# Mixer A, prompt: two chunks of keys scored at once by two 64-row tiles of TensorE, three products each

## The chip, the cores and the metric

The kernel runs on one core of one Trainium2 chip. The metric is the device time of one launch in microseconds (us). Before the change the median of three runs is 1541.89 us (1539.67 to 1544.26).

## The reference, cut to what matters

Two token sequences, a prompt of 1024 and a sample of 512, pass through two layers with shared weights. In the first layer mixer A is dense attention with 8 query heads on 2 groups of keys and values, 64 numbers per head:

```python
def dense_gqa(q, k, v):
    ...
    def attend(qblk):
        s = jnp.einsum('bqkgd,bskd->bkgqs', qblk, k).astype(F32)
        p = jax.nn.softmax(s, axis=-1).astype(v.dtype)
        return jnp.einsum('bkgqs,bskd->bqkgd', p, v)
```

A block of 128 queries sees all keys of its own sequence: 1024 in the prompt, 512 in the sample. Everything is in 32-bit floats.

## The kernel before

**Two parts per number.** TensorE takes 32-bit data in a fast form (F32R) that keeps fewer bits. So the kernel splits an operand into a high part and a low part and adds products of parts. A projection with weights `w` and tokens `x` takes three F32R products per step (`proj_fm_k`): high by high, high by low, low by high.

**Scores of mixer A.** A head has 64 numbers, and the array of TensorE has 128 rows. The kernel stacks: the tile K of a key group (`ak`) holds the high part of the keys on partitions 0 to 63 and the low part on 64 to 127, and the query tiles `qh` and `ql` hold the high and the low part of a head twice, once per half. The product of `qh` with K is then high by high plus high by low, and that of `ql` with K the two others. So 512 keys cost two matmuls on all 128 rows.

**Units.** A unit is one block of 128 queries of one key group, with 4 heads. There are 2 groups and 12 blocks, the four of the sample first and then the eight of the prompt, for the first group and then for the second. `front_a` (L763) makes a unit's scores and exponentials. For a prompt block there are two chunks of 512 keys per head (`nh` is 2); each chunk takes one PSUM bank `s`, two matmuls (recorded at L89, the helper `mm`) and a row maximum on VectorE (L782). Then the smaller of the two negated maxima is taken (L787), ScalarE makes the exponentials (L790), VectorE the sums and their reciprocals (L792, L793), and GpSimd scales the exponentials (L107). The `yield` between the chunks ends a step of the pipeline.

**Products with the values.** `Back.T` (L628) transposes four blocks of exponentials into a bank `pte` (L170) and splits them into `eh` (ScalarE, L111) and `el` (VectorE, L112); `Back.PV` (L636) multiplies them with the values into `po`.

**The order of the work.** `pipeline` (L673) writes the program's order: after the transposes of a key block it takes as many steps of later units' `front_a` as the 12 exponential buffers and a credit allow, then some `fill` pieces, then the products of the key block before. Fills are the query projections of the second group (`psq`), the gate projections (`psg`), and later the out projection (`pso`). When the program is built, a scheduler puts the instructions of each engine into their final order: by priority, which follows the program's order, but an instruction whose buffer is not yet free in the scheduler's own clock waits aside while others go ahead. The five PSUM banks with tag `s` serve the scores, the transposes `pte` and the query transposes `ptq` alike.

**K in DRAM.** `kv_group` (L458) writes each key group to DRAM as 128 rows, high over low, 1024 keys wide for the prompt. `load_a` (L756) brings it back with one DMA from GpSimd's queue (L760).

**Another use of a half array.** In mixer B the scores `pss` are 32-bit products with 64 rows (`kT` by `qT`, four products of 128 columns, each recorded as two instructions); the products `kv` and mixer B's `po` beside them have the same columns on 128 rows. `b_proj` makes its projections `psb` (256 columns, F32R, 128 rows).

Of the kernel before, what the change touches and what calls it, by code (L numbers as in the profile page):

```python
# [9 lines left out]
F32R = mybir.dt.float32r  # L10
AF = mybir.ActivationFunctionType
ALU = mybir.AluOpType
AX = mybir.AxisListType
# [3 lines left out]
P = 128  # L17
# [19 lines left out]
def trunk_kernel(ctx, tc, x, xT, wab, woab, wc, woc, gT, qkg, ret, sink, relb, fng,  # L37
                 ropeA, ropeB, dist, kdist, qdist, onehot, wmask, out_p0, out_p1, out_s):
    nc = tc.nc
# [13 lines left out]
    def buf(tag, name, n=None, dt=F32):  # L53
        t = wk.tile([P, SIZE[tag]], dt, tag=tag, name=name, bufs=BUFS[tag])
        return t if n is None else t[:, :n]

    def ps_s(name):
        return pp.tile([P, 512], F32, tag="s", name=name, bufs=5)
# [14 lines left out]
    def small(name, n, bufs=2):  # L73
        return st.tile([P, n], F32, tag=name, name=name, bufs=bufs)
# [13 lines left out]
    def mm(ps, lhsT, rhs, start, stop):  # L88
        i = nc.tensor.matmul(ps, lhsT=lhsT, rhs=rhs, start=start, stop=stop)  # L89
        if pace["after"] is not None:  # L90
            tc.add_manual_dep(i.ins, pace["after"], order, reason="a filler keeps to its place in the pipeline")
            pace["after"] = None
        return i
# [12 lines left out]
    def scale_pool(o, i, s):  # L106
        nc.gpsimd.tensor_scalar(o, i, s, 1.0, ALU.mult, ALU.mult)  # L107
# [22 lines left out]
    def load_w(arr, c, tag, lo=None, hook=None, ks=range(KT)):  # L130
        ts = {}
        for i in (k // 2 for k in ks[::2]):
            raw = wp.tile([P, 2 * CW], F32, tag="wraw", name="wraw", bufs=2)
            dma(out=raw, in_=arr[c, :, 2 * i:2 * i + 2, :].rearrange("p k n -> p (k n)"))
            w = wp.tile([P, 2, 2 * CW], F32R, tag=tag, name=tag, bufs=4)
            nc.gpsimd.tensor_scalar(w[:, 0, :], raw, 1.0, 1.0, ALU.mult, ALU.mult)  # L136
            (lo or nc.gpsimd).tensor_tensor(w[:, 1, :], raw, w[:, 0, :].bitcast(F32), ALU.subtract)  # L137
            ts[i] = w
            if hook is not None:
                hook(i)  # L140

        def get(s, k, a=0, n=CW):
            o = (k % 2) * CW + a
            return ts[k // 2][:, s, o:o + n]
        return get
# [183 lines left out]
    def scratch(name):  # L329
# [8 lines left out]
    sp_d = {(n, g, i): dr.tile([P, 1024 if i == 0 else 512], F32, name=f"sp{n}{g}{i}")[:]  # L338
            for n in ("ak", "av", "ch", "cl", "cv") for g in range(2) for i in range(2)}

# [1 line left out]
    ident = const.tile([P, P], F32, name="ident")  # L342
    make_identity(nc, ident)
    nhalf = const.tile([P, 8], F32, name="nhalf")
# [16 lines left out]
        for b in range(t * GB, t * GB + GB):  # L361
            block_rstd(load_block(x[b], "xb", "H"), rs[:, b:b + 1])

# [1 line left out]
    dma(out=g_sb, in_=gT)  # L365
    nc.scalar.activation(rs, rs, AF.Tanh)
    wkv = load_w(wab, 4, "w", None, lambda i: [load_xt(0, k) for k in ((0, 1), (2, 3, 4, 5), (6, 7), ())[i]])
# [127 lines left out]
        if p % 2:  # L495
            kv_group(p // 2)

# [1 line left out]
    ropeb = buf("S4", "ropeb").rearrange("p (f b d) -> p f b d", f=2, b=8)  # L499
    dma(out=ropeb, in_=ropeB)  # L500
    qdec = buf("S4", "qdec").rearrange("p (h a i) -> p h a i", h=4, a=2)
# [116 lines left out]
            tail, last = retention(h, w, b0, b1), tail  # L618
            last()

# [1 line left out]
    class Back:  # L622
        def __init__(self, eget, n, vget, od, k0, t, j, gd):
            self.n, self.eget, self.vget, self.od, self.k0, self.t, self.j = n, eget, vget, od, k0, t, j
# [46 lines left out]
                split(X["h", k, self.t][:, sl], X["l", k, self.t][:, sl], oT[:, a, :], 0.5)  # L671

    def pipeline(units, prep, front, cap, frees, rate, fill, hook, before=None):  # L673
        """Software pipeline: the scores of later units run beside the products of this one, as far as
        the buffers of the exponentials (cap of them) reach."""
        n = len(units)
        st_ = dict(u=0, gen=None, live=0)
        ctxs, backs, pend = {0: prep(units[0])}, {}, []

        def advance():  # L680
            u = st_["u"]
            if u >= n:
                return False
            if st_["gen"] is None:
                st_["gen"] = front(units[u], ctxs.pop(u))
                if u + 1 < n:
                    ctxs[u + 1] = prep(units[u + 1])
                st_["need"] = next(st_["gen"])
            if st_["live"] + st_["need"] > cap:
                return False  # L690
            st_["live"] += st_["need"]
            try:
                st_["need"] = next(st_["gen"])
            except StopIteration as e:
                backs[u] = e.value
                st_["u"], st_["gen"] = u + 1, None
            return True

        credit = 0.0
        for u in range(n):  # L700
            while u not in backs:
                advance()
                if before is not None and backs:
                    before()
                    before = None
            back = backs.pop(u)
            for kb in range(back.n):
                back.T(kb)
                st_["live"] -= frees(kb, back.n)
                credit = min(credit + rate(back.n), 4.0)  # L710
                while credit >= 1.0 and advance():
                    credit -= 1.0
                fill.step()
                for f in pend:
                    f()
                pend = [lambda bk=back, kb=kb: bk.PV(kb)]
                if kb == 0:
                    hook(units[u])
        for f in pend:
            f()  # L720
# [33 lines left out]
    kv_a = {}  # L754

    def load_a(name, g, b):  # L756
        i = 0 if b < 8 else 1
        if (name, g, i) not in kv_a:
            kv_a[name, g, i] = buf(("S4", "S2")[i], name, None, F32R)
            nc.gpsimd.dma_start(out=kv_a[name, g, i], in_=sp_d[name, g, i])  # L760
        return kv_a[name, g, i]

    def front_a(u, ctx):  # L763
        g, b = u
        qh, ql = ctx
        t, j = b // GB, b % GB
        s0, s1 = (0, 8) if b < 8 else (8, 12)
        nh = (s1 - s0) // GB
        K = load_a("ak", g, b)
        nm, rl = small("nm", 4), small("rl", 4)  # L770
        l = small("l", 8).rearrange("p (h c) -> p h c", h=4)
        es = []
        for h in range(4):
            yield nh
            ss = []
            nm2 = small("nm2", 2, 4)
            for c in range(nh):
                kk = K[:, c * 512:(c + 1) * 512]
                s = ps_s("s")
                mm(s, qh[:, h * P:(h + 1) * P], kk, True, False)  # L780
                mm(s, ql[:, h * P:(h + 1) * P], kk, False, True)
                nc.vector.tensor_reduce(nm2[:, c:c + 1] if nh == 2 else nm[:, h:h + 1], s, AX.X, ALU.max, negate=True)  # L782
                ss.append(s)
                if c < nh - 1:
                    yield 0
            if nh == 2:
                nc.vector.tensor_tensor(nm[:, h:h + 1], nm2[:, 0:1], nm2[:, 1:2], ALU.min)  # L787
            eh = [buf("E", "e") for c in range(nh)]
            for c in range(nh):
                nc.scalar.activation(eh[c], ss[c], AF.Exp, bias=nm[:, h:h + 1], accum_out=l[:, h, c:c + 1])  # L790
            if nh == 2:
                nc.vector.tensor_tensor(rl[:, h:h + 1], l[:, h, 0:1], l[:, h, 1:2], ALU.add)  # L792
                nc.vector.reciprocal(rl[:, h:h + 1], rl[:, h:h + 1])  # L793
            else:
                nc.vector.reciprocal(rl[:, h:h + 1], l[:, h, 0:1])
            for c in range(nh):
                scale_pool(eh[c], eh[c], rl[:, h:h + 1])
            es.append(eh)
        return Back(lambda h, kb: es[h][kb // 4][:, (kb % 4) * P:(kb % 4 + 1) * P], s1 - s0,
                    lambda kb: load_a("av", g, b)[:, kb * P:(kb + 1) * P], o_ab, 2 * g, t, j,  # L800
                    g_ab if g == 1 and t < 2 else None)

# [1 line left out]
    def fin_fm(t, k, y, rb):  # L804
        nc.gpsimd.tensor_tensor(y, y, rb, ALU.mult)
        split_x(y, k, t, g_sb[:, KT + k:KT + k + 1])
# [22 lines left out]
    def begin():  # L829
# [3 lines left out]
        for _ in range(POST_A):  # L833
            fill.one()

    pipeline([(g, b) for g in range(2) for b in BLOCKS], prep_a, front_a, BUFS["E"],
             lambda kb, n: 4 if kb % 4 == 3 else 0, lambda n: 2.0, fill, hook_a, begin)
    drain(ahead)
# [11 lines left out]

    out_proj(1, woab, KS_A, lambda b: x[b], fin_ab)

# [1 line left out]
    wkv = load_w(wc, 0, "w")  # L854
    kd_raw = {}
    for p in PAIRS:
# [34 lines left out]
            split(q[r0:r0 + 64], q[r1:r1 + 64], ps[r0:r0 + 64], 0.125)  # L891
        yield

# [1 line left out]
    k_c, v_c = {0: (KH, KL)}, {0: (V,)}  # L895
    qs = {}
    bias_c = {}
# [104 lines left out]
        return Back(lambda h, kb: es[h][:, kb * P:(kb + 1) * P], k1 - k0, lambda kb: vget_c(c, k0 + kb), o_c, 2 * c, t, j,  # L1002
                    g_c if (c, t) == (3, 1) else None)

# [1 line left out]
    def fin_out(t, k, y, rb):  # L1006
        nc.vector.scalar_tensor_tensor(y, y, g_sb[:, 2 * KT + k:2 * KT + k + 1], rb, ALU.mult, ALU.mult)
        dma(out=(out_p0, None, out_s)[t][k], in_=y)
# [126 lines left out]
```

## Time and profile before

| | |
|---|---|
| median of 3 runs | 1541.89 us (1539.67 to 1544.26) |
| span of the profiled execution | 1541.9 us |
| TensorE matmul busy | 1467.9 us, 95% of the span |
| VectorE busy | 1061.1 us, 69% |
| GpSimd busy | 804.7 us, 52% |
| ScalarE busy | 714.0 us, 46% |
| mean granted TensorE clock | 0.985 |

Times are device microseconds. The profiled execution is one run of its own; its span agrees with the median of the timed runs. PE is TensorE's matmuls and PEld its weight loads, which run beside them; DVE is VectorE, ACT ScalarE, POOL GpSimd. Matmuls are pipelined: a 512-column matmul is shown with 0.39 us, of which neighbours overlap, so that the distance from start to start is the time that one costs. A shape such as 64\*128 in a row is the rows and columns of the array that an instruction uses.

### The profile page before, as it was taken

Reading aid. Unit: us, or ns where it says so; the run is one execution under the profiler, and the core shown is the slowest. Engines: PE = TensorE matmul, PEld = TensorE weight load, DVE = VectorE, ACT = ScalarE, POOL = GpSimd, SP = SyncE. Lnnn points to the kernel's source line nnn. Section 1 sums busy time; section 2 is a strip of 40 time slices with the busy share of each in tenths; the row PEclk is TensorE's granted clock in tenths of the full one; section 3 lists DMA queues with packets and bytes.
Section 4 is the critical chain, followed back from the end, with each engine's and each line's share of the span. In section 5 each row is a group of like instructions: output and inputs, shape, how many; then the busy total and the mean of one; then the engine's idle time right before and its main releaser. Section 6 shows DMA issues by size and latency. Waiting matters only on the chain.

```text
span 1541.9 us, 26034 instructions
## 1 busy us (share of the span) xinstructions
PE 1467.9 (95%) x8746; PEld 1277.2 (83%) x8746; DVE 1061.1 (69%) x2488; ACT 714.0 (46%) x1768; POOL 804.7 (52%) x1040
## 2 busy tenths in 40 slices
PE   7989999989999999999998999999999999988897
PEld 7988999987888888778777998888888888766677
DVE  6596455578667667877888327677777767898554
ACT  3632222245455555655653235556556556555102
POOL 7783334257456374887896414442522432567433
PEclk9998999999999999999999999999999999999999
DMA  9441011224421132654563422112213211567773
GB/s 334 155 154 52 19 45 49 64 85 140 138 73 59 48 110 73 217 166 130 153 218 115 124 78 78 52 57 56 80 49 93 61 53 52 169 211 235 242 247 123
DMA packets 112662, 179.54 MB, mean 116 GB/s; under 512 B 12880, under 2 KB 34000, under 8 KB 112528
## 3 DMA queue, kind: packets, MB, share of 16 engines
q1 hardware_dynamic: 110512, 172.37, 35.6%
q0 software_dynamic: 2016, 5.51, 1.2%
q8 instruction: 69, 1.13, 0.3%
q14 instruction: 65, 0.53, 0.1%
HBM read 125.63 MB, written 56.39 MB: 118 GB/s over the span
## 4 chain that ended last, share of the span: by engine, by line
PE 65%; DVE 12%; DMA 8%; POOL 5%; issue 4%; ACT 2%; SPq 1%; POOLq 0%; DVEq 0%; ACTq 0%
PE psg L89 16%; PE psq L89 10%; PE psb L89 8%; PE po L89 8%; PE pte L170 6%; PE pso L89 4%; PE sc L89 3%; PE s L89 3%; PE pskv L89 2%; DMA wraw<-in_woc 2%; DVE xl L118 1%; DVE w L137 1%; DVE nm L782 1%; DMA wraw<-in_woab 1%; DVE el L112 1%
## 5 line engine op out<-in xcount | busy, mean ns | idle before, releaser
L89 PE MATMUL psg<-xh,wg 128*128 128x512 f32 x768 | 261.6, 399 | 1.4 <-POOL wg L137 1.2
L112 DVE TENSOR_TENSOR el<-pte,eh 128x512 fp32r<-128x512 f32 x288 | 196.6, 684 | 56.7 <-ACT eh L111 29.6
L107 POOL TENSOR_SCALAR ec<-ec,rl 128x384 f32<-128x384 f32 (+1 forms) x192 | 109.0, 582 | 233.0 <-DVE rl L997 77.1
L111 ACT ACTIVATE eh<-pte 128x512 fp32r<-128x512 f32 x288 | 169.4, 596 | 119.6 <-PE po L89 66.4
L89 PE MATMUL pso<-xh,w 128*128 128x512 f32 x512 | 179.8, 409 | 9.8 <-DVE w L137 4.3
L89 PEld LDWEIGHTS psg<-xh,wg 128*128 128x128 f32 x768 | 143.7, 188 | 29.7 <-POOL wg L137 1.6
L107 POOL TENSOR_SCALAR e<-e,rl 128x512 f32<-128x512 f32 x160 | 114.6, 728 | 81.7 <-DVE rl L793 23.8
L89 PE MATMUL psg<-xl,wg 128*128 128x512 f32 x384 | 151.1, 393 | 0.0
L992 ACT ACTIVATE ec<-ec,nm 128x384 f32<-128x384 f32 (+1 forms) x192 | 109.6, 572 | 85.6 <-DVE nm L990 80.8
L790 ACT ACTIVATE e<-s,nm 128x512 f32<-128x512 f32 x160 | 108.9, 687 | 75.3 <-DVE nm L787 56.1
L136 POOL TENSOR_SCALAR w<-wraw 128x512 fp32r<-128x512 f32 x116 | 78.7, 680 | 117.7 <-DMA wraw<-in_woc 35.2
L782 DVE TENSOR_REDUCE nm<-s 128x1 f32<-128x512 f32 x160 | 107.5, 682 | 34.3 <-PE s L89 34.0
L89 PE MATMUL psq<-xh,w 128*128 128x512 f32 x384 | 130.1, 397 | 0.6 <-DVE oT L655 0.6
L89 PEld LDWEIGHTS pso<-xh,w 128*128 128x128 f32 x512 | 96.1, 191 | 34.7 <-DVE w L137 7.8
L986 DVE CUSTOM_DVE_ANT_0 ec<-sc,bias,sink_s 128x384 f32<-128x384 f32 (+1 forms) x192 | 105.2, 568 | 20.3 <-PE sc L89 17.4
L89 PE MATMUL pso<-xl,w 128*128 128x512 f32 x256 | 102.0, 399 | 3.3 <-DVE xl L118 3.3
L170 PEld LDWEIGHTS pte<-ident,e 128*128 128x128 f32 x640 | 78.4, 142 | 20.5 <-ACT e L790 1.7
L170 PE MATMUL pte<-ident,e 128*128 128x128 f32 x640 | 94.6, 275 | 0.8 <-ACT e L790 0.6
L137 POOL TENSOR_TENSOR w<-wraw,w 128x512 fp32r<-128x512 f32 x68 | 90.5, 1335 | 1.8
L89 PEld LDWEIGHTS psq<-xh,w 128*128 128x128 f32 x384 | 71.8, 188 | 14.4 <-PE po L89 0.9
L89 PEld LDWEIGHTS psg<-xl,wg 128*128 128x128 f32 x384 | 72.3, 188 | 13.2
L89 PE MATMUL pskv<-w,xh 128*128 128x256 f32 x384 | 73.3, 293 | 9.0 <-ACT xh L117 6.7
(225 smaller groups left out, 3981.8 us busy)
## 6 DMA issues: line engine op xcount, KB each, us to landing
wraw<-in_woab SPq DMA_DIRECT2D x48, 256.0 KB, 3.3
wraw<-in_woc SPq DMA_DIRECT2D x48, 256.0 KB, 3.6
wraw<-in_wab SPq DMA_DIRECT2D x44, 256.0 KB, 3.3
wraw<-in_wc SPq DMA_DIRECT2D x36, 256.0 KB, 3.2
xt<-in_xT SPq DMA_DIRECT2D x24, 256.0 KB, 5.3
xb<-in_x SPq DMA_DIRECT2D x24, 256.0 KB, 4.9
qd<-qdw SPq DMA_DIRECT2D x24, 256.0 KB, 2.0
qd<-qd SPq DMA_DIRECT2D x24, 256.0 KB, 3.1
```

Of the source, the lines that this page charges most:

```text
L89: i = nc.tensor.matmul(ps, lhsT=lhsT, rhs=rhs, start=start, stop=stop)
L107: nc.gpsimd.tensor_scalar(o, i, s, 1.0, ALU.mult, ALU.mult)
L111: nc.scalar.activation(hi, src, AF.Copy)
L112: nc.vector.tensor_tensor(lo, src, hi.bitcast(F32), ALU.subtract)
L118: nc.vector.scalar_tensor_tensor(lo, src, scale, hi.bitcast(F32), ALU.mult, ALU.subtract)
L136: nc.gpsimd.tensor_scalar(w[:, 0, :], raw, 1.0, 1.0, ALU.mult, ALU.mult)
L137: (lo or nc.gpsimd).tensor_tensor(w[:, 1, :], raw, w[:, 0, :].bitcast(F32), ALU.subtract)
L170: return nc.tensor.transpose(o, i, ident)
L782: nc.vector.tensor_reduce(nm2[:, c:c + 1] if nh == 2 else nm[:, h:h + 1], s, AX.X, ALU.max, negate=True)
L790: nc.scalar.activation(eh[c], ss[c], AF.Exp, bias=nm[:, h:h + 1], accum_out=l[:, h, c:c + 1])
L986: nc.vector.tensor_tensor_reduce(es[h][:, :nk], s, bias[h][:, bo:bo + nk], 1.0, sink_s[:, 4 * c + h:4 * c + h + 1], ALU.add, ALU.max, mx[: ...
L992: nc.scalar.activation(es[a][:, :nk], es[a][:, :nk], AF.Exp, bias=nm[:, a:a + 1], accum_out=l[:, a:a + 1])
```

## The change

For prompt blocks the K tile holds one chunk of 512 keys on partitions 0 to 63 and the other on 64 to 127, each with its high part (index 0) and its low part (index 1) side by side. Four DMAs of 64 rows by 512 keys replace one. A head then takes both banks at the start and issues six matmuls of 64 rows, alternating between the two halves of the array: high by high, high by low, low by high for each chunk. The fourth product, low by low, is left out for the prompt. Both maxima follow, and the `yield` between the chunks is gone. Sample blocks stay as they were.

```diff
     def load_a(name, g, b):
         i = 0 if b < 8 else 1
         if (name, g, i) not in kv_a:
-            kv_a[name, g, i] = buf(("S4", "S2")[i], name, None, F32R)
-            nc.gpsimd.dma_start(out=kv_a[name, g, i], in_=sp_d[name, g, i])
+            src = sp_d[name, g, i]
+            if name == "ak" and i == 0:
+
+                kk = buf("S4", name, None, F32R).rearrange("p (s k) -> p s k", s=2)
+                for r in range(2):
+                    for s in range(2):
+                        nc.gpsimd.dma_start(out=kk[64 * r:64 * r + 64, s, :],
+                                            in_=src[64 * s:64 * s + 64, 512 * r:512 * r + 512])
+                kv_a[name, g, i] = kk
+            else:
+                kv_a[name, g, i] = buf(("S4", "S2")[i], name, None, F32R)
+                nc.gpsimd.dma_start(out=kv_a[name, g, i], in_=src)
         return kv_a[name, g, i]
...
         for h in range(4):
             yield nh
-            ss = []
-            nm2 = small("nm2", 2, 4)
-            for c in range(nh):
-                kk = K[:, c * 512:(c + 1) * 512]
-                s = ps_s("s")
-                mm(s, qh[:, h * P:(h + 1) * P], kk, True, False)
-                mm(s, ql[:, h * P:(h + 1) * P], kk, False, True)
-                nc.vector.tensor_reduce(nm2[:, c:c + 1] if nh == 2 else nm[:, h:h + 1], s, AX.X, ALU.max, negate=True)
-                ss.append(s)
-                if c < nh - 1:
-                    yield 0
+            hs = slice(h * P, (h + 1) * P)
+            ss = [ps_s("s") for c in range(nh)]
             if nh == 2:
+
+                for n, (q, kl) in enumerate(((qh, 0), (qh, 1), (ql, 0))):
+                    for c in range(2):
+                        rows = slice(64 * c, 64 * c + 64)
+                        mm(ss[c], q[rows, hs], K[rows, kl, :], n == 0, n == 2)
+                nm2 = small("nm2", 2, 4)
+                for c in range(2):
+                    nc.vector.tensor_reduce(nm2[:, c:c + 1], ss[c], AX.X, ALU.max, negate=True)
                 nc.vector.tensor_tensor(nm[:, h:h + 1], nm2[:, 0:1], nm2[:, 1:2], ALU.min)
+            else:
+                mm(ss[0], qh[:, hs], K, True, False)
+                mm(ss[0], ql[:, hs], K, False, True)
+                nc.vector.tensor_reduce(nm[:, h:h + 1], ss[0], AX.X, ALU.max, negate=True)
```

The other hunks of the diff only turn comment lines and a docstring into blank lines.

## Rows read from the trace of the kernel before

**Rows 1.** The page, part 1: TensorE's busy time, share of the span, instructions.

```profile
PE 1467.9 (95%) x8746; PEld 1277.2 (83%) x8746; DVE 1061.1 (69%) x2488; ACT 714.0 (46%) x1768; POOL 804.7 (52%) x1040
```

**Rows 2.** Busy time by stretch: length, five engines, granted clock, DMA share, GB/s.

```profile
358.00:400.00 42.00, 38.88 (x201) 30.65 (x201) 29.96 (x70) 18.51 (x43) 22.56 (x28) 1.00 0.70 205
400.00:545.00 145.00, 143.85 (x734) 118.36 (x733) 97.31 (x203) 77.09 (x174) 76.04 (x94) 1.00 0.18 58
...
597.00:700.00 103.00, 97.27 (x483) 78.16 (x483) 83.53 (x150) 58.59 (x130) 74.76 (x78) 0.98 0.50 157
700.00:796.00 96.00, 93.86 (x474) 74.47 (x473) 81.47 (x155) 55.80 (x127) 81.33 (x86) 1.00 0.52 155
```

**Rows 3.** Chain of waits from 400 to 545 us, shares by line.

```profile
by line: PE psg L89 49.9%; PE s L89 14.8%; PE pte L170 14.5%; PE po L89 13.8%; DMA gab<-gz 10.8%; PE ptq L170 1.8%; DVE nm L787 1.6%; DVE nm L782 1.0%; issue 0.9%; ACT e L790 0.7%; ACT eh L111 0.4%; ACT th L213 0.0%; ACTq L213 0.0%
```

**Rows 4.** Tile s: count, duration ns min/median/max, first and last start us, forms.

```profile
L89 PE MATMUL s<-ak,qh x160: 387/395/796, 319.4 to 793.4; 128*128 128x512 f32 x160
...
L89 PE MATMUL s<-ak,ql x160: 387/394/628, 319.7 to 793.7; 128*128 128x512 f32 x160
L782 DVE TENSOR_REDUCE nm<-s x160: 661/681/693, 320.2 to 796.7; 128x1 f32<-128x512 f32 x160
```

**Rows 5.** Timeline of PE, two heads of one unit: start us, us, what.

```profile
423.84 0.39 PE L89 MATMUL s<-ak,qh 128*128 128x512 f32 x1
424.07 0.39 PE L89 MATMUL s<-ak,ql 128*128 128x512 f32 x1
424.30 0.63 PE L89 MATMUL psg<-xh,wg 128*128 128x512 f32 x2
...
425.69 0.39 PE L89 MATMUL s<-ak,qh 128*128 128x512 f32 x1
...
427.53 0.39 PE L89 MATMUL s<-ak,qh 128*128 128x512 f32 x1
```

**Rows 6.** Timeline of PE: first and last prompt head, starts of both chunks.

```profile
358.51 0.39 PE L89 MATMUL s<-ak,qh 128*128 128x512 f32 x1
...
358.98 0.39 PE L89 MATMUL s<-ak,qh 128*128 128x512 f32 x1
...
791.76 0.40 PE L89 MATMUL s<-ak,qh 128*128 128x512 f32 x1
...
793.38 0.50 PE L89 MATMUL s<-ak,qh 128*128 128x512 f32 x1 [0.22 <-DVE el L112]
```

**Rows 7.** Timeline of PE, mixer B, 180 to 185 us, around the 64-row products.

```profile
180.38 0.28 PE L89 MATMUL psb<-wg,xh 128*128 128x256 f32 x1
180.50 1.05 PE L89 MATMUL kv<-z,kfb 128*128 128x128 f32 x8
...
183.10 0.36 PE L89 MATMUL psb<-wg,xh 128*128 128x256 f32 x1
183.30 0.28 PE L89 MATMUL psb<-wg,xl 128*128 128x256 f32 x1
183.42 0.29 PE L89 MATMUL psb<-wg,xh 128*128 128x256 f32 x1
183.63 1.16 PE L89 MATMUL pss<-qT,kT 64*128 64x128 f32 x8
184.72 0.39 PE L89 MATMUL psb<-wg,xh 128*128 128x256 f32 x1
184.94 0.28 PE L89 MATMUL psb<-wg,xl 128*128 128x256 f32 x1
```

**Rows 8.** Timeline of PE's weight loads at the same place.

```profile
183.30 0.19 PEld L89 LDWEIGHTS psb<-wg,xh 128*128 128x128 f32 x1
183.63 0.96 PEld L89 LDWEIGHTS pss<-qT,kT 64*128 64x128 f32 x8
```

**Rows 9.** Tile pss: all 64-row products of mixer B.

```profile
L89 PE MATMUL pss<-qT,kT x96: 272/272/579, 122.9 to 298.4; 64*128 64x128 f32 x96
```

**Rows 10.** Tile ak: its loads, duration ns, first and last start us.

```profile
L760 POOL DMA_DIRECT2D ak<-spak x4: 540/628/771, 281.7 to 548.5; - x4
```

## The prediction

> **What bounds the kernel now.** I read the page first: TensorE's matmuls fill 95% of the span and no other engine passes 69% [rows 1]. Then the four stretches in which the prompt's scores of mixer A run: TensorE is busy 38.88 of 42 us, 143.85 of 145, 97.27 of 103 and 93.86 of 96, so only 3.1, 1.2, 5.7 and 2.1 us are idle, 12.1 in all [rows 2]. The chain of waits in the longest of them is nearly all TensorE, with the scores at 14.8% [rows 3]. So here a microsecond of TensorE's time is about a microsecond of the kernel, as long as it isn't put into that idle time. What counts is the distance from one matmul's start to the next, not the 0.39 us of one: in the timeline 512-column products follow each other every 0.23 us [rows 5].
>
> The trace has no pair of row tiles, but it has matmuls on half the rows. In mixer B eight instructions of 64 rows stand between projections of 128 rows [rows 7]. From the start of the last projection before them (183.42) to the start of the second one after them (184.94) are 1.52 us. The control stands just ahead: from 180.38 to 183.30 the same kind of projections enclose 24 instructions of the same 128 columns on 128 rows (the 8 shown and the 16 of `po`), in 2.92 us. A projection of 256 columns takes 0.12 us there (180.38 to 180.50, 183.30 to 183.42), so one of the 24 takes (2.92 - 2 x 0.12) / 24 = 0.112 us, with no extra at either end. Eight of 64 rows and two projections should take 8 x 0.112 + 2 x 0.12 = 1.13 us; they took 1.52. **A round trip from 128 rows to 64 and back costs 0.39 us.** The weight loads show where: up to there each is pulled ahead of its matmul, but after the load at 183.30 the first one of 64 rows starts only at 183.63, with its matmul [rows 8]. There are twelve such groups (96 instructions) [rows 9], always with projections around them. I call any such run of 64-row matmuls an island.
>
> **What the change removes and adds.** 16 prompt units of 4 heads are 64 heads, and each loses four full matmuls (of the 320 recorded [rows 4], 256 go): 4 x 0.23 = 0.92 us a head. Each gets six 64-row matmuls instead, three per chunk.
>
> *Do two tiles run at the same time?* No row shows it. The bounds are 0.23 us for a pair (full overlap) and 0.46 (none). I take overlap, since the operands lie on different rows and different banks, and add 0.11 us a head, because the second tile's weights are loaded behind the first's: the eight loads of 64 rows follow each other every (0.96 - 0.19) / 7 = 0.11 us [rows 8]. The Trainium skill ("TensorE: Matmul & The Clock Gate", Part 3) puts the offset of two tiles at some 4 ns instead. By that the sum below would be 24 x 0.11 = 2.6 us less, within its range.
>
> *Do a head's six stand together?* The program has them in one piece, but the scheduler lets an instruction whose bank isn't free wait aside while later ones go on. The first product of the second chunk needs a second bank; the other two of the first chunk don't. So where the second bank comes late, the first chunk's three products run alone, then projections, then the second chunk's three: nothing overlaps and there are two islands. How late it comes is seen in the order of before, which also asks for both chunks in one go: the chunks of two heads start at 423.84, 425.69, 427.53 and so on, with projections between [rows 5]. I measured the distance from chunk to chunk over all 64 heads, from the first (358.51 to 358.98) to the last (791.76 to 793.38) [rows 6]: 24 are within 1.0 us, and 40 lie 1.1 to 5.3 us apart. An island of three takes about 0.3 us to enter and 0.69 to run, so I take the 24 as together and the 40 as split. The bounds are all together and all split.
>
> Prices a head: together 3 x 0.23 + 0.11 + 0.39 = 1.19, which is 0.27 more than 0.92; split 2 x (3 x 0.23 + 0.39) = 2.16, which is 1.24 more. The price of an island is from 32-bit products of 128 columns. For F32R of 512 columns it could lie between nothing (rival 3) and 0.50 us, if the engine has to run empty and a matmul of 512 columns lasts 0.11 us longer than one of 256 (0.39 [rows 5] against 0.28 [rows 7]); over 24 + 80 islands that would be 11 us more. I take 0.39, since the projections around it are F32R and the control shows no extra for the change of type alone.
>
> **Sum:** 24 x 0.27 + 40 x 1.24 = 6.5 + 49.6 = 56 us more on TensorE. Of the 12.1 us idle I let half be filled: -6 (bounds 0 and -12). That is +50 us on the profiled 1541.9 us, which is also the median of the runs (1541.89): **1592 us**.
>
> **Edits costed at nothing.** The two more loads per product change nothing of their own: they are in the pitch. K for the prompt comes in four DMAs instead of one, twice, so six more issues at 0.63 us on GpSimd's queue, 3.8 us [rows 10]; behind them wait the scalings of the exponentials. GpSimd is idle in at least 15% of each stretch [rows 2] and the last load of K was issued at 548.5, some 50 us ahead of the stretch at 597 that uses it. Uncovered it would be the 3.8 us, plus a transfer at most. Both row maxima (0.68 us each [rows 4]) now come behind the third pair, so the exponentials start later by some 0.3 us a head; the scores run half a unit ahead of the transposes, with projections to fill. Without that cover it is 64 x 0.3 = 19 us. The lost `yield` moves no step: the credit of four took both chunks in one go before.
>
> **Rivals.**
> 1. *All heads together, pairs overlapping.* For it: the six are adjacent in the program. Against it: the chunks' distances [rows 5, 6]. 64 x 0.27 = 17 us, less 6: 1553 us (1547 to 1559). Still slower, since the island costs more than the saved slot.
> 2. *Tiles don't overlap.* A head together takes 6 x 0.23 + 0.39 = 1.77, 0.85 more; split heads stay. 24 x 0.85 + 49.6 - 6 = +64: 1606 us, at most 1621 (64 x 1.24, nothing filled).
> 3. *Faster.* The saved slot shows and the islands don't cost: three pairs plus 0.11 against four, 0.12 us a head, or 0.23 if the second load is hidden: 64 x that is 8 to 15 us, 1527 to 1534. It decides if a round trip costs under 0.12 (0.23) us between F32R matmuls of 512 columns and the six stay together. For it: the trace's price is from another type. Against it: rows 7 and the split. The Trainium skill ("TensorEngine Tiling", Theoretical Speedup) promises up to twice the speed for 64 rows, which would be this rival; but its Key Properties say that a change of tiling mode drains the engine, which is what rows 7 and 8 show.
> 4. *No change.* Heads A and B of a step are written one behind the other; if they make one island of twelve, 6 x 0.23 + 0.11 + 0.39 = 1.88 stands against 1.84: 32 x 0.04 = +1 us, 1543. Against it: they are 1.8 us apart now [rows 5].
>
> **How the numbers follow.** Forecast 0.50, with a range of its own from 1570 (24 split, all idle filled) to 1621 (all split, nothing filled). Rival 1: 0.20, rival 2: 0.14, rival 3: 0.09, rival 4: 0.07. Under 0.3% (4.6 us, about what a measurement of this kernel can tell) only rival 4 is the same: faster 0.09, same 0.07, slower 0.84. The range leaves out rivals 3 and 4 and reaches from 1550, within rival 1, to 1621, the top of the forecast and of rival 2.
>
> **What would show it.** Right: in the timeline of PE three 64-row products `s` in a row on one half, then projections, then three on the other; ahead of each island a weight load that starts with its matmul, some 0.2 us late; over 30 heads with two islands; TensorE busy in the same stretches with fewer units done. Pairs that start 0.1 us apart and last 0.39 show overlap; 0.23 apart, none. Wrong: islands of six everywhere (rival 1), or no late load at the borders (rival 3), or the time lost on another engine, in waits for K or for the maxima.

## The result and the profile after

The change made the kernel slower: 1596.3 us (median of 4 runs, 1593.75 to 1597.19) against 1543.08 us for the kernel before, run beside it. The ratio is 1.0347, with a 95% interval of 1.0332 to 1.0363: 53 us, where +50 was forecast (1592 us, range 1550 to 1621).

The page of the changed kernel answers to [rows 1]: TensorE's matmuls are busy 63 us longer (1467.9 before), the other engines within 7 us of before.

```profile
span 1592.0 us, 26324 instructions
...
PE 1530.9 (96%) x8874; PEld 1282.0 (81%) x8874; DVE 1054.4 (66%) x2488; ACT 715.2 (45%) x1768; POOL 807.8 (51%) x1046
```

The time was lost where the scores are made. Below are the stretches from mixer A's first scores to its last product with the values, first in the kernel before (320 to 831 us), then in the changed one (320 to 885); the columns are those of [rows 2].

```profile
320.00:831.00 511.00, 490.66 (x2565) 402.05 (x2564) 383.19 (x763) 276.48 (x623) 338.26 (x383) 0.99 0.41 127
```

```profile
320.00:885.00 565.00, 554.09 (x2684) 406.93 (x2685) 380.41 (x763) 278.20 (x623) 339.89 (x385) 0.99 0.36 115
```

TensorE is busy 63.4 us longer and idle 10.9 us instead of 20.3, so 9.4 us went into idle time and the stretch is 54 us longer. Behind it some 4 us come back (710.9 us to the end before, 707 after). The granted clock is the same (0.99).

The timeline of PE in the changed kernel, where one head's second chunk stands alone between other work (an island of three products on half the rows):

```profile
373.92 0.39 PE L89 MATMUL psg<-xh,wg 128*128 128x512 f32 x1
374.15 0.40 PE L89 MATMUL psg<-xl,wg 128*128 128x512 f32 x1
374.48 0.73 PE L89 MATMUL s<-ak,qh 64*128 64x512 f32 x2
375.05 0.39 PE L89 MATMUL s<-ak,ql 64*128 64x512 f32 x1
375.38 0.50 PE L89 MATMUL po<-el,av 128*128 128x512 f32 x1
375.72 0.40 PE L89 MATMUL po<-eh,av 128*128 128x512 f32 x1
```

From the last full product before it (374.15) to the second one behind it (375.72) are 1.57 us, for five products at 0.23: 0.42 us is left over. Over the 56 islands of three that stand between full products like this one, the median of what one takes is 1.09 us, three products and 0.39. That is the price worked out in mixer B [rows 7], here between F32R products of 512 columns.

Where a head stayed together, six products take no longer than three:

```profile
637.10 0.40 PE L89 MATMUL po<-el,av 128*128 128x512 f32 x1
637.43 0.74 PE L89 MATMUL s<-ak,qh 64*128 64x512 f32 x4
638.00 0.40 PE L89 MATMUL s<-ak,ql 64*128 64x512 f32 x2
638.33 0.50 PE L89 MATMUL psg<-xh,wg 128*128 128x512 f32 x1
638.67 0.39 PE L89 MATMUL psg<-xl,wg 128*128 128x512 f32 x1
```

Again 1.57 us from 637.10 to 638.67, now with six products between. Four of them fit into 0.74 us: the two tiles overlap fully, the second starting 0.01 us behind the first. (The run on all rows, below, shows something more about this head: in TensorE's order the second chunk's three products stand behind the first chunk's three.) The weight loads of the same place show the border, as in [rows 8]:

```profile
636.88 0.19 PEld L89 LDWEIGHTS po<-el,av 128*128 128x128 f32 x1
637.43 0.30 PEld L89 LDWEIGHTS s<-ak,qh 64*128 64x128 f32 x4 [0.36 <-PE po L89]
637.77 0.19 PEld L89 LDWEIGHTS s<-ak,ql 64*128 64x128 f32 x2
638.33 0.19 PEld L89 LDWEIGHTS psg<-xh,wg 128*128 128x128 f32 x1 [0.36 <-DVE rl L806]
```

The loads stand still for 0.36 us ahead of the island and again behind it; elsewhere they run ahead of their matmuls. I counted the islands in the timeline: 125, of which 79 have three products, 9 have six, 2 more than six and the other 35 one, two, four or five. So of 64 heads only about one in seven stayed whole.

### The profile page after: what moved, and what is told of

Read it like the earlier page. It is cut to its first block, busy times and chain, and to the rows that moved or that the text cites. A ratio compares the mean times of both kernels' runs of the same rounds, so it can differ in the third digit from the quotient of the medians.

```text
span 1592.0 us, 26324 instructions
## 1 busy us (share of the span) xinstructions
PE 1530.9 (96%) x8874; PEld 1282.0 (81%) x8874; DVE 1054.4 (66%) x2488; ACT 715.2 (45%) x1768; POOL 807.8 (51%) x1046
## 4 chain that ended last, share of the span: by engine, by line
PE 75%; DVE 8%; DMA 6%; issue 2%; POOL 2%; ACT 1%; SPq 0%; POOLq 0%; DVEq 0%; ACTq 0%
PE psg L89 17%; PE psq L89 10%; PE po L89 10%; PE pso L89 9%; PE psb L89 8%; PE pte L170 7%; PE s L89 7%; PE sc L89 3%; PE pskv L89 2%; DMA wraw<-in_woc 1%; DMA mo<-gc 1%; DVE xl L118 1%; PE ptq L170 1%; DVE w L137 1%; PE pss L89 1%
## 5 line engine op out<-in xcount | busy, mean ns | idle before, releaser
L795 DVE TENSOR_REDUCE nm<-s 128x1 f32<-128x512 f32 x128 | 86.5, 686 | 58.8 <-PE s L89 57.5
L89 PE MATMUL s<-ak,qh 64*128 64x512 f32 (+1 forms) x288 | 97.6, 443 | 0.0
```

The costliest lines, as they stand in the source:

```text
L795: nc.vector.tensor_reduce(nm2[:, c:c + 1], ss[c], AX.X, ALU.max, negate=True)
```

## The experiments

Theory: TensorE's time is what counts, and it is lost by islands (0.39 us each) and by a third product that nothing overlaps, because the second chunk's bank comes late. The rivals: the order of work, the late maxima, the four DMAs, or waiting for banks.

**The same order on all rows.** The six products of a head use 128 rows; TensorE's instructions stand in exactly the order of the changed kernel. Left out is the separation of the chunks: each product sums over the rows of both.

```diff
-                        mm(ss[c], q[rows, hs], K[rows, kl, :], n == 0, n == 2)
+                        mm(ss[c], q[:, hs], K[:, kl, :], n == 0, n == 2)
```

> The changed kernel with its six products per head on all 128 rows of the array; TensorE's order of work is the same, instruction by instruction. It leaves the split into chunks out of the products (each sums over both chunks' rows), so only its time counts. Theory (islands): no weight load is late any more, TensorE has 128 more full products than before, 128 x 0.23 = 29 us, of which some 6 go into idle time: about 1566 us (1560 to 1573). Rival (the third product, the new order or late maxima cost the time, not the change of rows): as the changed kernel, 1590 to 1600.

Measured: 1567.66 us, ratio to the kernel before 1.0144 (1.0126 to 1.0162). The islands, net of the products that overlap in them, cost 1.0347 - 1.0144 = 2.0%, 31 us. The stretch of mixer A in this run:

```profile
320.00:857.30 537.30, 518.13 (x2695) 427.93 (x2694) 381.43 (x765) 277.16 (x623) 340.29 (x386) 0.99 0.39 121
```

TensorE is busy 36 us less than in the changed kernel, with the same instructions in the same order. 125 islands at 0.39 are 49 us. Of the 13 us between, overlapping products gave back some 10: in the changed kernel 45 products start beside another one and so save 0.23 us each. The rest is not accounted for. The 31 us are uncertain by some 4 on either side, and the two profiled executions, one of each kernel, differ by 22 us of span only (1592.0 and 1570.1).

On 128 rows the products start 0.23 us apart, one behind another, so this trace shows TensorE's order within a head. Here is the whole head that stood at 637.43 us in the changed kernel:

```profile
618.08 0.40 PE L89 MATMUL po<-el,av 128*128 128x512 f32 x1
618.31 0.62 PE L89 MATMUL s<-ak,qh 128*128 128x512 f32 x2
618.77 0.39 PE L89 MATMUL s<-ak,ql 128*128 128x512 f32 x1
619.00 0.61 PE L89 MATMUL s<-ak,qh 128*128 128x512 f32 x2
619.45 0.40 PE L89 MATMUL s<-ak,ql 128*128 128x512 f32 x1
619.69 0.39 PE L89 MATMUL psg<-xh,wg 128*128 128x512 f32 x1
```

The first chunk's three products come first and the second chunk's three behind them; the scheduler did not keep the program's alternation. In the changed kernel the second chunk's first product nevertheless starts 0.01 us after the first chunk's first, ahead of two products that precede it in TensorE's order. Six of the nine islands of six have this order, three alternate, and all take the same time (0.89 to 0.90 us from the first product to the full product behind them). So it is not the alternation that makes the tiles overlap.

**Each head in one piece.** A product of 2 columns takes the second bank first; the six follow in a fixed order, with higher priority.

```diff
+                first = mm(ss[1][:, 0:2], qh[:, hs], K[:, 0, 0:2], True, True)
...
-                        mm(ss[c], q[rows, hs], K[rows, kl, :], n == 0, n == 2)
+                        with tc.high_priority(offset=400 if (n, c) != (0, 0) else 0):
+                            i = mm(ss[c], q[rows, hs], K[rows, kl, :], n == 0, n == 2)
+                        tc.add_manual_dep(i.ins, first.ins.name, order, reason="both banks first")
+                        first = i
```

> The changed kernel with the six products of every prompt head in one piece: a product of 2 columns takes the second bank first, and the six follow each other by added order. Theory: 64 islands of six instead of 125 of mixed length. An island of six took 1.10 us in the changed kernel against 0.93 for the four products before, so 64 x 0.17 = 11 us, and 64 products of 2 columns at 0.11 = 7 us, less some idle time: about 1555 us (1548 to 1563), still slower than before. Rival (it is the waiting for banks, and taking two at once makes it worse): 1590 or more.

Measured: 1559.14 us, ratio 1.0087 (1.0072 to 1.0103). There are 64 islands, all of six, at a median of 1.10 us. This is rival 1 of the prediction made to happen: whole heads, full overlap, and still 13 us slower than before. But not all of the 13 us belong to the islands: the 64 products of 2 columns, which the change itself doesn't have, are some 7 us of work, and the new order of the scores costs 5 to 7 us without any tiles (below). That one head is too little work to pay for a round trip rests on the trace: an island of six takes 1.10 us, the four products before took 0.93. How much slower whole heads alone would be was not measured.

**The round trip alone.** In the kernel before, each prompt chunk gets a product of 2 columns ahead of it, on 64 rows in one run and on 128 rows in the other; TensorE's order is the same in both.

```diff
+                if nh == 2:
+                    mm(s[:, 0:2], qh[0:64, h * P:(h + 1) * P], kk[0:64, 0:2], True, True)
                 mm(s, qh[:, h * P:(h + 1) * P], kk, True, False)
```

> The kernel before, with one product of 64 rows and 2 columns ahead of each of the 128 prompt chunks, overwritten by the chunk's own. Theory: each is an island of one between F32R products of 512 columns and pays the round trip of 0.39 us and its own load of 0.11: 128 x 0.50 = 64 us, less some 10 of idle time: about 1597 us (1585 to 1607). Rival (the price belongs to the 32-bit products of mixer B): as the same visit on 128 rows.

> The same visit of 2 columns on 128 rows; TensorE's order is the same as in the run with 64 rows. Both theories: only the load, 128 x 0.11 = 14 us at most, some of it in idle time: 1548 to 1558 us. The difference to the run with 64 rows is the price of the round trip alone: 128 x 0.39 = 50 us by the theory, 0 by the rival.

Measured: 1584.16 us (ratio 1.0254, 1.0228 to 1.0280) with 64 rows and 1556.14 us (1.0078, 1.0056 to 1.0100) with 128. The difference, 1.8% or 27 us, has the theory's sign but half its size. The timelines of PE, first with 64 rows and then with 128 (each visit is merged with the chunk's first product):

```profile
473.32 0.40 PE L89 MATMUL psg<-xh,wg 128*128 128x512 f32 x1
473.64 0.70 PE L89 MATMUL s<-ak,qh 64*128 64x2 f32 x2
474.18 0.40 PE L89 MATMUL s<-ak,ql 128*128 128x512 f32 x1
```

```profile
460.53 0.40 PE L89 MATMUL psg<-xh,wg 128*128 128x512 f32 x1
460.77 0.51 PE L89 MATMUL s<-ak,qh 128*128 128x2 f32 x2
461.12 0.39 PE L89 MATMUL s<-ak,ql 128*128 128x512 f32 x1
```

From the projection's start to the chunk's second product are 0.86 and 0.59 us; without the two full products at 0.23 a visit takes 0.40 and 0.13; the medians of the visits that stand between full products are 0.40 and 0.11. So the 0.39 already holds the load of the island's first weights, which I had added once more: the price over a visit on 128 rows is 0.29, times 128 is 37 us, and TensorE's idle time in the stretch took some 6 of it (14 us idle with 64 rows, 20 with 128). That leaves 31 us; measured are 27, or 22 to 32 by the intervals. The profiled executions, one of each, differ by 36 us (1588.1 and 1551.6 of span). The rival, no price between F32R products, is out.

**All but the tiles.** The products of the kernel before, with everything else of the change.

```diff
-                kk = buf("S4", name, None, F32R).rearrange("p (s k) -> p s k", s=2)
+                kk = buf("S4", name, None, F32R)
                 for r in range(2):
                     for s in range(2):
-                        nc.gpsimd.dma_start(out=kk[64 * r:64 * r + 64, s, :],
+                        nc.gpsimd.dma_start(out=kk[64 * s:64 * s + 64, 512 * r:512 * r + 512],
...
-                for n, (q, kl) in enumerate(((qh, 0), (qh, 1), (ql, 0))):
-                    for c in range(2):
-                        rows = slice(64 * c, 64 * c + 64)
-                        mm(ss[c], q[rows, hs], K[rows, kl, :], n == 0, n == 2)
+                for c in range(2):
+                    mm(ss[c], qh[:, hs], K[:, 512 * c:512 * c + 512], True, False)
+                    mm(ss[c], ql[:, hs], K[:, 512 * c:512 * c + 512], False, True)
```

> Everything of the change but the tiles: K in four DMAs, no yield between the chunks, both banks taken in the program ahead of the products, both maxima behind them; the products are those of the kernel before, two per chunk on 128 rows. Theory (only products and islands cost): as the kernel before, within 5 us. Rival (the lost yield, the four DMAs on GpSimd's queue or the late maxima cost a part of the 53 us): 1550 or more.

Measured: 1551.49 us, ratio 1.0044 (1.0031 to 1.0057). The theory falls here: 7 us, not nothing. Two more runs tell whether the DMAs or the order did it. The first edits the kernel before as shown; the second is the run above with `load_a` of the kernel before.

```diff
-            kv_a[name, g, i] = buf(("S4", "S2")[i], name, None, F32R)
-            nc.gpsimd.dma_start(out=kv_a[name, g, i], in_=sp_d[name, g, i])
+            kv_a[name, g, i] = kk = buf(("S4", "S2")[i], name, None, F32R)
+            src = sp_d[name, g, i]
+            if name == "ak" and i == 0:
+                for r in range(2):
+                    for s in range(2):
+                        nc.gpsimd.dma_start(out=kk[64 * s:64 * s + 64, 512 * r:512 * r + 512],
+                                            in_=src[64 * s:64 * s + 64, 512 * r:512 * r + 512])
+            else:
+                nc.gpsimd.dma_start(out=kk, in_=src)
```

> The kernel before, with the prompt's K of mixer A loaded by four DMAs of 64 rows by 512 keys instead of one; the layout and the products stay. Theory (the queue of GpSimd has room): as the kernel before, within 3 us. Rival (six more issues hold back the scalings of the exponentials): the 7 us by which the run of the change without tiles was slower, or most of them.

> The change without tiles and without the four DMAs: only the lost yield, the banks named first and both maxima behind the products. Theory (the order costs what the run of the change without tiles lost): 5 to 9 us above the kernel before. Rival (the DMAs do): as the kernel before, within 3 us.

The four DMAs alone: 1545.62 us, ratio 1.0002 (0.9989 to 1.0016), nothing. The other part alone: 1552.29 us, ratio 1.0035 (1.0017 to 1.0052). So the 5 to 7 us belong to the new order of the scores. The stretch of mixer A in the run without tiles has 494.71 us of TensorE in 517.90, against 490.66 in 511:

```profile
320.00:837.90 517.90, 494.71 (x2549) 404.98 (x2549) 378.13 (x763) 277.40 (x620) 339.23 (x385) 0.98 0.41 125
```

The lost `yield` is unlikely to be what does it: between two groups of transposes `pte` as many products `s` stand in this trace as in the kernel before and in the changed one (for the prompt, two heads behind every fourth key block, none behind the others), so no head moved to another step. The banks named first and the late maxima were not taken apart.

**What splits the heads.** The changed kernel with a higher priority for a head's second to sixth product, so that only a missing bank can hold one back.

```diff
-                        mm(ss[c], q[rows, hs], K[rows, kl, :], n == 0, n == 2)
+                        with tc.high_priority(offset=400 if (n, c) != (0, 0) else 0):
+                            mm(ss[c], q[rows, hs], K[rows, kl, :], n == 0, n == 2)
```

> The changed kernel with a higher priority for the second to sixth product of a prompt head and no other edit, so nothing but a missing bank can hold one of them back. Theory (a late second bank splits the heads): most islands stay islands of three, 109 instead of 125; 16 islands fewer at 0.39 and some more overlap, 1578 to 1592 us. Rival (other work of higher priority splits them): nearly all heads in one piece, 1550 to 1562 us.

Measured: 1595.77 us, ratio 1.0326 (1.0310 to 1.0343). 89 islands of three are left, 18 of six and one of nine. So priority is out, and by exclusion it is the missing second bank that splits the heads; it fits that all heads stayed whole when that bank was taken first. But the time missed the expected range: 17 islands fewer gave at most some 3 us (ratios 1.0326 and 1.0347, whose intervals overlap), where 4 to 18 were expected. TensorE is busy 6.4 us less in the stretch (554.09 in the changed kernel) and idle 3.1 us more (10.9).

```profile
320.00:881.70 561.70, 547.70 (x2707) 405.22 (x2705) 380.99 (x764) 279.02 (x624) 340.18 (x386) 0.99 0.38 116
```

The profiled run is 2.1 us shorter than that of the changed kernel (1589.9 against 1592.0 us of span).

**Two heads in one island.** Four banks are taken first, then twelve products follow (the loop over `h` becomes one over pairs of heads).

```diff
+                        if (h, c) != (h0, 0):
+                            i = mm(sss[h][c][:, 0:2], qh[:, h * P:(h + 1) * P], K[:, 0, 0:2], True, True)
...
+                            with tc.high_priority(offset=400 if (h, n, c) != (h0, 0, 0) else 0):
+                                i = mm(sss[h][c], q[rows, hs], K[rows, kl, :], n == 0, n == 2)
+                            tc.add_manual_dep(i.ins, prev.ins.name, order, reason="four banks first")
```

> Two heads in one island: four banks are taken first, by three products of 2 columns on 128 rows, then twelve 64-row products in a row. Theory (the round trip is paid per island): 32 x (6 x 0.23 + 0.39 - 8 x 0.23) = -2 us, and 96 products of 2 columns at 0.11 = 10 us: about 1552 us (1545 to 1558), below the 1559 of one head per island. Rival (four of five banks at once starve the transposes): 1560 or more, with TensorE idle in the stretch.

Measured: 1587.66 us, ratio 1.0274 (1.0257 to 1.0291), so the rival was right. There are 32 islands of twelve, at a median of 1.87 us (1.79 by the sum), and TensorE's work is small: 512.04 us. But it is idle for 46 us:

```profile
320.00:878.50 558.50, 512.04 (x2803) 408.33 (x2802) 376.72 (x765) 277.45 (x624) 339.69 (x387) 0.97 0.38 117
```

The waits of PE in that stretch (us in total, times, longest) name what is late: the transposes wait for a bank. The exponentials that the waiting ones read had been ready for 18 us or more. What ended each of the 16 waits was an exponential that had finished reading the scores in the very bank of tag `s` that the transposes were to write. In the kernel before this wait took 0.6 us in all.

```profile
PE pte L170 <- ACT e L819: 24.6, 16, 3.3
PE pto L170 <- DVE on L591: 5.2, 1, 5.2
PE pte L170 <- DVE ql L112: 3.6, 1, 3.6
```

**The kernel before without its own islands.** If the price is general, the twelve groups of mixer B on which the prediction rested must pay it too. Their operands get 128 rows, with zeros under `kT`.

```diff
-            qT, kT = v4(buf("H", "qT"))[:64], v4(buf("H", "kT"))[:64]
-            nc.scalar.activation(qT, pt[0:64], AF.Copy)
+            qTf, kTf = v4(buf("H", "qT")), v4(buf("H", "kT"))
+            qT, kT = qTf[:64], kTf[:64]
+            nc.gpsimd.memset(kTf[64:128], 0.0)
+            nc.scalar.activation(qTf, pt, AF.Copy)
             nc.scalar.activation(kT, pt[64:128], AF.Copy)
...
-                i = mm(pss[:, j, :], kT[:, j, :], qT[:, j, :], True, True)
+                i = mm(pss[:, j, :], kTf[:, j, :], qTf[:, j, :], True, True)
```

> The kernel before without its own islands: mixer B's twelve groups of 64-row products get their operands on 128 rows, with zeros under kT (a memset on GpSimd) and the other half of the same transposed tile under qT; the values stay the same. Theory (each island costs 0.39 us wherever it stands): 12 x 0.39 = 4.7 us less where TensorE is busy without a gap, so 3 to 5 us faster than the kernel before. Rival (the 0.39 belongs to something else in these groups): no change, or slower by the memsets.

Measured: 1539.24 us against 1545.84 for the kernel before, ratio 0.9964 (0.9947 to 0.9981): by the ratio 5.6 us faster (2.9 to 8.2), and the fastest of all versions here. The timeline of PE at the place of [rows 7]:

```profile
182.78 0.28 PE L89 MATMUL psb<-wg,xh 128*128 128x256 f32 x1
182.90 1.05 PE L89 MATMUL pss<-qT,kT 128*128 128x128 f32 x8
183.71 0.36 PE L89 MATMUL psb<-wg,xh 128*128 128x256 f32 x1
183.91 0.28 PE L89 MATMUL psb<-wg,xl 128*128 128x256 f32 x1
```

From 182.78 to 183.91 are 1.13 us, the number that the prediction gave for eight such products without a border; with 64 rows it was 1.52. Ten of the twelve groups stand between projections of 256 columns and give up their border: 1.51 to 1.53 us before, 1.13 now, 3.9 us in all. The first has `kv` ahead of it, so the prediction's "always with projections around them" is not quite right; the last gained nothing (1.57 and 1.56 us), because TensorE then waits for ScalarE behind it.

## Why the prediction was right, point by point

- **TensorE is the bound.** Right: 63.4 us more work made the stretch 54 us longer.
- **0.39 us for an island.** Right, and carried over from 32-bit products of 128 columns to F32R of 512. Three runs bear on it: 31 us for the islands of the changed kernel by the run on full rows, 27 us for the visits, 5.6 us won in mixer B. The run with whole heads shows the price in its islands (1.10 us), not in its time alone.
- **Split heads.** Right in kind, too mild in number. I took 24 heads as whole and 80 islands for the others, 104 in all; there are 125, and only some nine heads stayed whole. A distance under 1.0 us was too generous a sign of a head that stays together: of the 24, only five had nothing between their chunks in the kernel before (0.46 to 0.47 us). That the late second bank is the cause follows from the run with added priority, by exclusion, and fits the run with the bank taken first, which also fixed the order.
- **The tiles overlap.** Right. My 0.11 us for the second tile's load was wrong: it is 0.01, or less where the halves alternate. It counted only in the heads that stayed together, 24 x 0.11 = 2.6 us in the sum. Here the Trainium skill ("TensorE: Matmul & The Clock Gate", Part 3), with its some 4 ns, was nearer.
- **Idle time.** I let 6 of 12.1 us be filled; it was 9.4, of 20.3 us in the longer stretch measured above.
- **Edits costed at nothing.** The four DMAs, right. The new order of the scores, wrong: without any tiles it costs 5 to 7 us. That the lost `yield` moves no step holds in the traces. So what failed is that the pipeline covers the late maxima, or that naming both banks ahead of the products, for which I had no term, costs nothing; which of the two stays open.

The runs in a row give the parts: 0.44% (7 us) without tiles, 1.44% with the third products on full rows, 3.47% with the islands. So the third products add some 15 us (12 to 19 by the intervals) of the 128 x 0.23 = 29 us of work they are, and the islands 31 us (28 to 35); the profiled executions alone, one of each, would say 23 and 22. Term by term, the forecast was 56 us of TensorE's work less 6 of idle time; measured were 63 less 9, and some 4 us that came back behind the stretch. That +50 meets +53 so closely owes something to errors that cancel: more islands (125 for 104) and fewer overlapping products (45 for 72) on one side, more idle time filled and the 4 us behind the stretch on the other. Counted from the trace, 125 x 0.39 + (128 - 45) x 0.23 is 68 us of work, 5 more than measured; that difference isn't explained. How much of the order's 7 us is still there in the changed kernel, where its waits may hide behind TensorE's own work, stays open.

## What to carry to other kernels

Two row tiles do run at the same time, but going from 128 rows to 64 and back costs TensorE 0.39 us, as much as 1.7 products of 512 columns. A tiled piece must save more than that before other work comes between its matmuls; count the border for each run of tiled matmuls in the final order, not for each call in the program, and look whether the scheduler can keep the run together with the PSUM banks it has. Where a few matmuls on half the rows stand among full ones, filling the other half with zeros can be cheaper than leaving it out.

## What the runs showed of the hardware that was not expected

Products of 64 rows in F32R overlap fully in pairs: six took the 1.10 us of three, border included. They did so whether the two halves alternated in TensorE's order or one half's three products stood behind the other's three: then the second half's first product started 0.01 us after the first half's first, ahead of two products that precede it in the order. The border's 0.39 us already holds the load of the island's first weights: an island with one product of 2 columns takes 0.40 us, against 0.11 for the same product on 128 rows (medians).
